# Key norms from turned keys, a value factor on ScalarE and a head factor on GpSimd in a hybrid decoder block

## The chip, the cores and the metric

The kernel runs on one core of a Trainium2 chip. A core has a matrix engine (TensorE, PE in the profile, with its weight loads as PEld), VectorE (DVE), ScalarE (ACT), GpSimd (POOL) and SyncE (SP), which only issues transfers. The metric is the device time of one execution in microseconds.

## The reference

One decoder layer of two token mixers on 512 tokens of width 2048, all in float32. The input is normed to `u`; one projection of `u` gives everything that both mixers need. The first mixer (mLSTM, 8 heads) is not touched here. The second is a gated DeltaNet with 16 heads of 128 channels. Queries, keys and values go through a short causal convolution and SiLU, and queries and keys are divided by their norms. Per head, in chunks:

```
kk    = k k^T
a_mat = strict_lower(beta_t * kk * decay)
sol   = (I + a_mat)^-1 [ v*beta , k*beta*exp(gam) ]
step:   u = w_val - w_k S ;  o = q_dec S + (q k^T * decay) u ;  S = g_end S + k_end^T u
```

The norms of the keys enter `a_mat` and the right-hand side as factors per token. Both mixers' outputs go through a norm and gates, one output projection, a gated sum with the input and a last norm.

## The kernel before, in words

The 32-bit products are split: a weight tile is cast to a high part on ScalarE (`split_hi`, L140), the low part is the difference on VectorE (`split_lo`, L143), and PE runs three matmuls for each pair. Up to L796 the kernel makes most of the projection; after it, eight units (`dn_unit`, L1128) of two heads each run the key, value and query projection of those heads (`proj_cm`, L246). The output projection follows (`wide_block`, then `seven` and `last_block`).

All other work is woven between the projections by Python generators. `tick()` is called after each group of six projection matmuls, 48 times in a unit, and every active generator that is due goes on to its next `yield n`, which says in how many ticks it wants to go on. So a `yield` sets where in PE's order, and in the program order of the other engines, a step stands. PE keeps the order of the program. The other engines' orders are laid out by a planner from a simulated timeline, with `urgent(level)` raising precedence and `behind("A")`, `behind("V")` or `behind("S")` putting an instruction after the newest split on ScalarE, the newest split on VectorE or the newest weight load on SyncE. At run time each engine goes through its list in order.

The steps of a unit that matter here:

- `silu_end` (L840) ends the SiLU of keys, values or queries and calls `turn` (L856), which transposes 32x32 blocks on VectorE and starts `travel` (L863): four writes to DRAM on SyncE's queue, and some ticks later one read back, which completes a transposed tile. The turned keys are `ke`, with tokens on partitions.
- `dn_front_k` (L882) makes decay matrices `dm`, the products `pk` of keys with keys (L915) and `aq` = `pk` * `dm` (L917). It takes the keys' squared norms `nk` from the diagonal of `aq` by four masked sums a head on VectorE (L920), forms `cs` = beta / `nk`, scales `aq` on ScalarE (L935 to L938) and `dm` on GpSimd (L946), sends 32x32 blocks through DRAM to `ls`, and inverts 32 triangular systems at a time in 31 steps of two VectorE instructions (L964, L966), two steps to a tick. The result `xi` goes through DRAM to `tt` (L979) and is turned to `tn` (L982).
- `dn_back` (L1006) builds the full 128x128 inverses in `tb` from 32x32 and 64x64 blocks by four groups of small matmuls, p1 (L1020), p2 (L1035, L1036), p3 (L1046, L1047) and p4 (L1056, L1057), with copies between them on VectorE, ScalarE and GpSimd (`ta` and `tb`). It also multiplies the values `vn` by the keys' norms (`nk`, by then their roots; L1029).
- `dn_chain` (L1065) walks the four chunks of a head, each a few matmuls with VectorE and ScalarE steps between.

`token_norms` (L849) is there already, for the queries:

```
for c in range(NC):
    with urgent():
        A.activation(jk, pk[:, c, :], AF.Square, accum_out=dst[:, c:c + 1])
```

Of the kernel before, what the change touches and what calls it, by code (L numbers as in the profile page):

```python
# [8 lines left out]
F32 = mybir.dt.float32  # L9
F32R = mybir.dt.float32r  # L10
AF = mybir.ActivationFunctionType
ALU = mybir.AluOpType
# [3 lines left out]
P = 128  # L16
S = 512
NC = S // P
# [28 lines left out]
UNITS = list(range(8))  # L47
# [11 lines left out]
def hybrid_body(  # L59
# [18 lines left out]
    V, A, G, T = nc.vector, nc.scalar, nc.gpsimd, nc.tensor  # L78
# [16 lines left out]
    ident = cp.tile([P, P], F32, tag="ident", name="ident")  # L95
# [49 lines left out]
    def behind(eng):  # L145

        return tc.issue_after(newest[eng])
# [65 lines left out]
    def start(gen, wait=0, by=None):  # L213
        active.append([gen, clock["t"] + wait, held["by"] if by is None else by])
# [79 lines left out]
    for c in range(NC):  # L294
        xt = xts[c]
        jk = p0.tile([P, HD], F32, tag="jk", name="jk", bufs=2)
# [524 lines left out]
    def bc(col, n):  # L821
        return col.unsqueeze(2).to_broadcast([P, NC, n])
# [17 lines left out]
    def silu_end(dst, then=None):  # L840
        th = wkb.tile([P, S], F32, tag="th", name="th", bufs=2)
        with behind("A"):
            A.activation(th, dst, AF.Tanh)
        V.scalar_tensor_tensor(out=dst, in0=th, scalar=1.0, in1=dst, op0=ALU.add, op1=ALU.mult)
        if then is not None:
            turn(*then)
        yield 1

    def token_norms(pk, dst):  # L849

        jk = wk.tile([P, P], F32, tag="jk", name="njk", bufs=1)
# [3 lines that stand above are left out]
# [8 lines left out]
    def travel(o, dst, out, apart):  # L863

        d = dst if len(dst.shape) == 4 else dr.tile([16, BS, 4, BS], F32, tag="td", name="td", bufs=8)
        ov = o.rearrange("p n (j c) -> p (n j) c", c=BS)
        if out:
            for a in range(4):
                with behind("A") if out is nc.scalar else ExitStack():
                    out.dma_start(d[:, :, a, :].rearrange("m r c -> r m c"), ov[a * BS:(a + 1) * BS])  # L870
                if apart:
                    yield 1
            return
        with urgent(2):
            for a in range(4):
                nc.sync.dma_start(d[:, :, a, :].rearrange("m r c -> r m c"), ov[a * BS:(a + 1) * BS])
        yield 4
        with urgent(2):
            nc.sync.dma_start(dst, d.rearrange("(n j) r a c -> (j r) n (a c)", n=NC))
        yield 1  # L880

    def dn_front_k(hs, kq, u):  # L882
# [26 lines left out]
        for j in range(2):  # L909
            aq = u["pool"].tile([P, NC, 2, P], F32, tag="aq", name="aq", bufs=2)  # L910
            u["aq"].append(aq)
            pk = psw.tile([P, NC, P], F32, tag="wk", name="pk")
            for c in range(NC):
                tsl = slice(c * P, (c + 1) * P)
                T.matmul(pk[:, c, :], kq[j][:, 0, tsl], kq[j][:, 0, tsl], start=True, stop=True)  # L915
            with urgent():
                V.tensor_tensor(out=aq[:, :, 0, :], in0=pk, in1=u["dm"][j][0], op=ALU.mult)  # L917
                jk = wkb.tile([P, P], F32, tag="jd", name="jd", bufs=1)
                for c in range(NC):
                    V.scalar_tensor_tensor(out=jk, in0=aq[:, c, 0, :], scalar=1.0, in1=ident, op0=ALU.mult,  # L920
                                           op1=ALU.mult, accum_out=nk[:, j, c:c + 1])
            yield 1
        V.tensor_scalar(out=nk, in0=nk, scalar1=EPS, scalar2=None, op0=ALU.add)
        V.reciprocal(cs, nk)
        for j in range(2):
            V.tensor_tensor(out=cs[:, j, :], in0=cs[:, j, :], in1=beta[:, :, hs[j]], op=ALU.mult)
        u["nk"], u["cs"] = nk, cs
        ld = dr.tile([2 * NC, 4, BS, BS], F32, tag="ld", name="ld", bufs=2)
        yield 3
        for j in range(2):  # L930
            aq = u["aq"][j]
            with behind("A"):
# [26 lines left out]
        for i in range(BS - 1):  # L959
            n, m = BS - 1 - i, i // 4 + 1  # L960
            tmp = wkb.tile([P, 80], F32, tag="tmp", name="tmp")
            tv = tmp[:, 0:n * m].rearrange("p (a b) -> p a b", b=n)
            with behind("V"):
                V.tensor_tensor(out=tv, in0=ls[:, i, i + 1:BS].unsqueeze(1).to_broadcast([P, m, n]),  # L964
                                in1=xi[:, 0:m, i].unsqueeze(2).to_broadcast([P, m, n]), op=ALU.mult)
            V.tensor_tensor(out=xi[:, 0:m, i + 1:BS], in0=xi[:, 0:m, i + 1:BS], in1=tv, op=ALU.subtract)  # L966
            if i % 2:
                yield 1
        for j in range(2):
            ke = u["ke"][j]  # L970
# [5 lines left out]
        with urgent():  # L976
            for q in range(4):
                nc.sync.dma_start(xd[:, :, :, q, :].rearrange("g b m t -> (g b) m t"), xi[q * NSYS:(q + 1) * NSYS])
            nc.sync.dma_start(tt, xd.rearrange("g b m q t -> (b m q) g t"))  # L979
        yield 16  # L980
        with urgent(), behind("V"):
            V.transpose(tn.rearrange("p g m -> p (g m)"), tt.rearrange("p g t -> p (g t)"))  # L982
        u.update(tn=tn, tt=tt)
# [22 lines left out]
    def dn_back(hs, kq, u):  # L1006

        tn, tt = u["tn"], u["tt"]
        G2 = [(j * NC + c, u["aq"][j][:, c, 0, :]) for j in range(2) for c in range(NC)]
        for b in range(4):  # L1010
            bs = slice(b * BS, (b + 1) * BS)
            G.tensor_copy(tb[bs, :, bs], tt[bs])
        for b in range(2):
            bs = slice(b * BS, (b + 1) * BS)
            G.tensor_copy(ta[bs, :, bs], tn[bs])
        p1 = psw.tile([P, 2 * NC, BS], F32, tag="wk", name="p1")
        for g, a in G2:
            for q in range(2):
                a0, a1 = slice(64 * q, 64 * q + 32), slice(64 * q + 32, 64 * q + 64)
                T.matmul(p1[a1, g, :], a[a0, a1], tn[a0, g, :], start=True, stop=True)  # L1020
        s1 = wk.tile([P, 2 * NC, BS], F32, tag="s3", name="s1", bufs=1)
        for q in range(2):
            a1 = slice(64 * q + 32, 64 * q + 64)
            with urgent():
                A.mul(s1[a1], p1[a1], -1.0)
        for j in range(2):
            vn = u["vs"][j]
            with behind("V"):
                V.tensor_tensor(out=vn, in0=vn, in1=bc(u["nk"][:, j, :], P), op=ALU.mult)  # L1029
        yield 2  # L1030
        p2 = psw.tile([P, 2, 2 * NC, BS], F32, tag="wk", name="p2")
        for g, a in G2:
            for q in range(2):
                a0, a1 = slice(64 * q, 64 * q + 32), slice(64 * q + 32, 64 * q + 64)
                T.matmul(p2[a0, 0, g, :], s1[a1, g, :], tt[a1, g, :], start=True, stop=True)  # L1035
            T.matmul(p2[32:64, 1, g, :], tt[32:64, g, :], s1[32:64, g, :], start=True, stop=True)  # L1036
        with urgent(2):
            V.tensor_copy(ta[32:64, :, 0:32], p2[32:64, 1])
        for q in range(2):
            a0, a1 = slice(64 * q, 64 * q + 32), slice(64 * q + 32, 64 * q + 64)  # L1040
            with urgent():
                A.copy(tb[a0, :, a1], p2[a0, 0])
        yield 3
        p3 = psw.tile([P, NC, 64], F32, tag="wk", name="p3")
        for c in range(NC):
            T.matmul(p3[64:128, c, :], G2[c][1][0:64, 64:128], ta[:, c, :], start=True, stop=True)  # L1046
            T.matmul(p3[0:64, c, :], G2[NC + c][1][64:128, 0:64], tb[64:128, NC + c, 64:128], start=True, stop=True)  # L1047
        s3 = wk.tile([P, NC, 64], F32, tag="s3", name="s3", bufs=1)
        with urgent():
            A.mul(s3[64:128], p3[64:128], -1.0)  # L1050
            V.tensor_tensor(out=s3[0:64], in0=p3[0:64], in1=u["cs"][0:64, 1, :].unsqueeze(2).to_broadcast([64, NC, 64]),
                            op=ALU.mult)
        yield 3
        p4 = psw.tile([P, NC, 64], F32, tag="wk", name="p4")
        for c in range(NC):
            T.matmul(p4[0:64, c, :], s3[64:128, c, :], tb[64:128, c, 64:128], start=True, stop=True)  # L1056
            T.matmul(p4[64:128, c, :], ta[:, NC + c, :], s3[0:64, c, :], start=True, stop=True)  # L1057
        with urgent():
            V.tensor_copy(tb[0:64, 0:NC, 64:128], p4[0:64])
            A.mul(tb[0:64, NC:2 * NC, 64:128], p4[64:128], -1.0)  # L1060
        soon = hs[0] == 2 * UNITS[-1]
        start(dn_chain(0, hs, kq, u, soon), 3 - soon)
        start(dn_chain(1, hs, kq, u, soon), 4 - soon)
# [64 lines left out]
    def dn_unit(p):  # L1128
# [7 lines left out]
        for j in range(2):  # L1136
            ke = u["pool"].tile([P, NC, P], F32, tag="ke", name="ke", bufs=2)
            u["ke"].append(ke)
            conv_silu(ps[j], 16 + hs[j], kq[j][:, 0, :])
            start(silu_end(kq[j][:, 0, :], (kq[j][:, 0, :], ke)), 4 + 3 * j, front)  # L1140
        start(dn_front_k(hs, kq, u), 1, front)
        ps = proj_cm(DN_V + dcol)
        for j in range(2):
# [641 lines left out]
```

## Time and profile before

| | us |
|---|---|
| median of three runs | 2145.11 |
| lowest and highest of them | 2144.95, 2146.8 |
| the profiled execution, its own time | 2143.23 |
| its span from first to last instruction | 2141.5 |
| PE busy | 2113.5 |
| VectorE busy | 1708.0 |
| ScalarE busy | 1057.6 |
| GpSimd busy | 451.1 |

The granted clock of PE was 0.998 of full speed. In the rows, a line number is that of the kernel, then come the engine, the operation, what it writes and reads, the shapes and a count; behind the first bar the busy time in us and the mean of one in ns, behind the second the idle time of the engine ahead of these instructions and what ended it. A row of waits names who waited for whom, with the total in us, how often and the longest. A row of a timeline begins with the time from the span's start and the duration, and has in brackets the engine's idle time ahead of it. A row of a window gives its length and for PE, PEld, DVE, ACT and POOL the busy time with the count of instructions, then the granted clock, the share of the transfer engines and GB/s. A row on one tile gives shortest, median and longest in ns.

### The profile page before, as it was taken

The numbers are of one execution on the slowest core, as the hardware profiler recorded it, in microseconds if no ns is written. First come the engines' busy times: TensorE is split into PE (matmuls) and PEld (weight loads), VectorE is DVE, ScalarE is ACT, GpSimd is POOL, SyncE is SP. The second block draws the span as 40 slices with busy tenths as digits, with TensorE's granted clock in tenths as the row PEclk, the third lists the DMA queues.
The fourth block names the chain that finished last, engine by engine and source line by source line (L and its number), as shares of the span: only waits on it lengthen the run. The fifth ranks groups of instructions, "written<-read, shape, count | busy, mean of one in ns | idle before, by whom it ended". The sixth has DMA issues, their size and how long they took to land.

```text
span 2141.5 us, 32018 instructions
## 1 busy us (share of the span) xinstructions
PE 2113.5 (99%) x10544; PEld 1752.6 (82%) x10544; DVE 1708.0 (80%) x2981; ACT 1057.6 (49%) x2066; POOL 451.1 (21%) x667
## 2 busy tenths in 40 slices
PE   6999999999999999999999999999999999999998
PEld 5888888888888888888888888888888888887886
DVE  5888888788788778777766887888878878569887
ACT  5444454445444444444445546456465464345345
POOL 0000000000004000000003335344343363233211
PEclk9999999999999999999999999999999999999999
DMA  5355676667677767766766867777686677778895
GB/s 162 119 192 190 212 217 198 220 199 224 206 234 237 245 196 226 240 209 212 253 205 165 208 166 180 183 180 192 182 211 173 171 189 224 196 223 287 245 302 225
DMA packets 447144, 444.21 MB, mean 207 GB/s; under 512 B 197121, under 2 KB 303842, under 8 KB 446850
## 3 DMA queue, kind: packets, MB, share of 16 engines
q1 hardware_dynamic: 377618, 337.22, 53.9%
q0 software_dynamic: 24752, 72.90, 10.9%
q10 hardware_dynamic: 44608, 32.06, 4.8%
q8 instruction: 82, 1.34, 0.3%
q14 instruction: 84, 0.69, 0.1%
HBM read 348.66 MB, written 97.58 MB: 208 GB/s over the span
## 4 chain that ended last, share of the span: by engine, by line
PE 95%; DVE 2%; DMA 2%; issue 1%; SPq 0%; POOL 0%; ACT 0%; DVEq 0%; POOLq 0%; ACTq 0%
PE ps L578 18%; PE ps L580 18%; PE ps L579 18%; PE pj L257 10%; PE pj L259 9%; PE pj L258 9%; PE py L1407 2%; PE py L1409 2%; PE py L1408 2%; PE pk L915 1%; DMA wr<-in_w_out_dram 1%; PE pqk L990 1%; PE pw L1087 1%; PE pnum L1213 1%; PE po L1102 1%
## 5 line engine op out<-in xcount | busy, mean ns | idle before, releaser
L143 DVE TENSOR_TENSOR wl<-wr,wh 128x512 fp32r<-128x512 f32 (+1 forms) x522 | 444.3, 852 | 176.5 <-ACT wh L140 172.3
L140 ACT CAST wh<-wr 128x512 fp32r<-128x512 f32 (+1 forms) x522 | 373.9, 717 | 422.1 <-PE pj L258 218.5
L257 PE MATMUL pj<-uh,wh 128*128 128x512 f32 x896 | 375.8, 419 | 0.0
L259 PE MATMUL pj<-uh,wl 128*128 128x512 f32 x896 | 351.5, 392 | 0.0
L258 PE MATMUL pj<-ul,wh 128*128 128x512 f32 x896 | 349.8, 390 | 0.0
L578 PE MATMUL ps<-wh,uh 128*128 128x512 f32 x752 | 292.7, 389 | 0.8 <-DVE X L632 0.8
L579 PE MATMUL ps<-wl,uh 128*128 128x512 f32 x752 | 292.6, 389 | 0.0
L580 PE MATMUL ps<-wh,ul 128*128 128x512 f32 x752 | 292.6, 389 | 0.0
L140 ACT CAST wh<-t 128x1024 fp32r<-128x1024 f32 x120 | 126.3, 1053 | 301.7 <-PE ps L580 197.5
L533 POOL DMA_DIRECT2D t_d<-ts x104 | 56.6, 544 | 921.8 <-DVE ts L520 853.5
L579 PE MATMUL ps<-wl,suh 128*128 128x512 f32 x624 | 242.9, 389 | 0.0
L580 PE MATMUL ps<-wh,sul 128*128 128x512 f32 x624 | 242.8, 389 | 0.0
L578 PE MATMUL ps<-wh,suh 128*128 128x512 f32 x624 | 242.8, 389 | 0.0
L140 ACT CAST wh<-ts 128x512 fp32r<-128x512 f32 x240 | 147.9, 616 | 184.7 <-DVE ts L538 157.6
L143 DVE TENSOR_TENSOR wl<-t,wh 128x1024 fp32r<-128x1024 f32 x120 | 147.0, 1225 | 81.9 <-ACT wh L140 81.5
L259 PEld LDWEIGHTS pj<-uh,wl 128*128 128x128 f32 x896 | 168.3, 188 | 37.0
L257 PEld LDWEIGHTS pj<-uh,wh 128*128 128x128 f32 x896 | 169.2, 189 | 29.7
L258 PEld LDWEIGHTS pj<-ul,wh 128*128 128x128 f32 x896 | 169.3, 189 | 28.5
L143 DVE TENSOR_TENSOR wl<-ts,wh 128x512 fp32r<-128x512 f32 x240 | 164.9, 687 | 32.6 <-ACT wh L140 31.2
L578 PEld LDWEIGHTS ps<-wh,uh 128*128 128x128 f32 x752 | 141.2, 188 | 30.4 <-DVE X L632 1.2
L579 PEld LDWEIGHTS ps<-wl,uh 128*128 128x128 f32 x752 | 141.2, 188 | 29.5
L580 PEld LDWEIGHTS ps<-wh,ul 128*128 128x128 f32 x752 | 141.2, 188 | 29.2
(345 smaller groups left out, 3804.2 us busy)
## 6 DMA issues: line engine op xcount, KB each, us to landing
wr<-in_w_in_dram SPq DMA_DIRECT2D x744, 256.0 KB, 3.6
wr<-in_w_out_dram SPq DMA_DIRECT2D x138, 256.0 KB, 4.8
t_d<-ts POOLq DMA_DIRECT2D x104, 256.0 KB, 3.6
wr<-t_d SPq DMA_DIRECT2D x104, 256.0 KB, 3.7
xt<-in_x_dram SPq DMA_DIRECT2D x8, 512.0 KB, 7.2
tg_d<-X ACTq DMA_DIRECT2D x16, 256.0 KB, 4.8
tg_d<-to ACTq DMA_DIRECT2D x16, 256.0 KB, 4.6
v<-v_d SPq DMA_DIRECT2D x8, 512.0 KB, 5.6
```

Of the source, the lines that this page charges most:

```text
L140: newest["A"] = A.copy(hi, src).ins
L143: newest["V"] = V.tensor_tensor(out=lo, in0=src, in1=hi.bitcast(F32), op=ALU.subtract).ins
L257: T.matmul(ps[j], hi[:, k, wsl], uh[:, kt, :], start=(kt == 0), stop=False)
L258: T.matmul(ps[j], hi[:, k, wsl], ul[:, kt, :], start=False, stop=False)
L259: T.matmul(ps[j], lo[:, k, wsl], uh[:, kt, :], start=False, stop=(kt == KT - 1))
L533: queue.dma_start(t2_d[b % 2, i], ts[:, 0, :])
L578: T.matmul(ps[t], ah, hi, start=(g == "A" and i == 0), stop=False, skip_group_check=True)
L579: T.matmul(ps[t], ah, lo, start=False, stop=False, skip_group_check=True)
L580: T.matmul(ps[t], al, hi, start=False, stop=(i == KH - 1), skip_group_check=True)
L1407: T.matmul(ps[c], uh[:, kt, tsl], hi, start=(kt == ks[0]), stop=False)
L1408: T.matmul(ps[c], uh[:, kt, tsl], lo, start=False, stop=False)
L1409: T.matmul(ps[c], ul[:, kt, tsl], hi, start=False, stop=(kt == ks[-1]))
```

## The change

Four things change, all in the units. The keys' squared norms no longer come from the diagonal of `aq` but from the turned keys `ke`, by `token_norms` on ScalarE, some ticks later; `cs` and the inverse move with them. In exchange the second head's silu end is started a tick earlier, the read in `travel` comes three ticks after the writes instead of four (for every turned tile that is read back), there are twelve ticks instead of sixteen from the inverse's way out to its turning, and in the last unit four steps of the inverse are issued to a tick. The values' factor goes from VectorE (two instructions) to ScalarE (eight). The second head's factor `cs` is put into the right half of `ta` by GpSimd before p4, instead of into p3's result by VectorE after p3; p3's result is then negated as a whole by ScalarE, and the sign of the last copy changes.

```diff
@@ travel
-        yield 4
+        yield 3
@@ dn_front_k
-                jk = wkb.tile([P, P], F32, tag="jd", name="jd", bufs=1)
-                for c in range(NC):
-                    V.scalar_tensor_tensor(out=jk, in0=aq[:, c, 0, :], scalar=1.0, in1=ident, op0=ALU.mult,
-                                           op1=ALU.mult, accum_out=nk[:, j, c:c + 1])
             yield 1
+        yield 2
+        for j in range(2):
+            with behind("A"):
+                token_norms(u["ke"][j], nk[:, j, :])
+            yield 2 - j
         V.tensor_scalar(out=nk, in0=nk, scalar1=EPS, scalar2=None, op0=ALU.add)
...
-        yield 3
+        yield 2
         for j in range(2):
             aq = u["aq"][j]
...
-            if i % 2:
+            if i % 4 == 3 or (i % 2 and hs[0] < 2 * UNITS[-1]):
                 yield 1
...
-        yield 16
+        yield 12
@@ dn_back
-            with behind("V"):
-                V.tensor_tensor(out=vn, in0=vn, in1=bc(u["nk"][:, j, :], P), op=ALU.mult)
+            with behind("A"):
+                for c in range(NC):
+                    A.mul(vn[:, c, :], vn[:, c, :], u["nk"][:, j, c:c + 1])
...
+        G.tensor_tensor(out=ta[:, NC:], in0=ta[:, NC:], in1=u["cs"][0:64, 1, :].unsqueeze(2).to_broadcast([64, NC, 64]),
+                        op=ALU.mult)
...
-            A.mul(s3[64:128], p3[64:128], -1.0)
-            V.tensor_tensor(out=s3[0:64], in0=p3[0:64], in1=u["cs"][0:64, 1, :].unsqueeze(2).to_broadcast([64, NC, 64]),
-                            op=ALU.mult)
+            A.mul(s3, p3, -1.0)
...
-            A.mul(tb[0:64, NC:2 * NC, 64:128], p4[64:128], -1.0)
+            A.copy(tb[0:64, NC:2 * NC, 64:128], p4[64:128])
@@ dn_unit
-            start(silu_end(kq[j][:, 0, :], (kq[j][:, 0, :], ke)), 4 + 3 * j, front)
+            start(silu_end(kq[j][:, 0, :], (kq[j][:, 0, :], ke)), 4 + 2 * j, front)
```

## The prediction

> **What bounds the kernel now.** I read the page's first part, then TensorE's (PE) waits, then the stages in windows, then who waits for whom in the weight path.
>
> ```profile
> span 2141.5 us, 32018 instructions
> PE 2113.5 (99%) x10544; PEld 1752.6 (82%) x10544; DVE 1708.0 (80%) x2981; ACT 1057.6 (49%) x2066; POOL 451.1 (21%) x667
> ...
> L143 DVE TENSOR_TENSOR wl<-wr,wh 128x512 fp32r<-128x512 f32 (+1 forms) x522 | 444.3, 852 | 176.5 <-ACT wh L140 172.3
> L140 ACT CAST wh<-wr 128x512 fp32r<-128x512 f32 (+1 forms) x522 | 373.9, 717 | 422.1 <-PE pj L258 218.5
> ```
>
> PE stands idle 2141.5 - 2113.5 = 28.0 us. Where:
>
> ```profile
> PE pprm L108 <- POOL rs L304: 14.6, 1, 14.6
> PE put L313 <- DVE xt L290: 2.1, 2, 1.3
> PE ps L578 <- DVE X L632: 0.8, 1, 0.8
> PE ps L578 <- DVE X L1431: 0.7, 2, 0.5
> PE pw L1087 <- DVE r L1082: 0.3, 1, 0.3
> ```
>
> ```profile
> 0.00:25.00 25.00, 8.33 (x38) 6.94 (x38) 13.89 (x29) 14.68 (x21) 3.26 (x14) 1.00 0.78 238
> 1204.00:1290.00 86.00, 85.70 (x529) 71.50 (x527) 72.56 (x194) 49.23 (x138) 29.95 (x45) 1.00 0.68 171
> 2130.00:2141.50 11.50, 2.08 (x10) 1.39 (x8) 4.43 (x10) 3.75 (x6) 1.08 (x2) 0.71 0.67 274
> ```
>
> The start holds 25.00 - 8.33 = 16.67 us, the last stretch 11.50 - 2.08 = 9.42 us. What is left is 28.0 - 16.67 - 9.42 = 1.91 us: 0.30 us in the eight DeltaNet units, which the change touches, and about 1.6 us where the output products begin. The change therefore works on engines that PE does not wait for. The two group rows say the same from the other side: ScalarE's weight split (L140) is held up mostly by PE giving buffers back (218.5 of its 422.1 us idle), so the splits run ahead as far as the buffers let them. Nothing in the units can be gained that PE does not lose now: the ceiling is 1.91 us, 0.09%.
>
> **The clock of the units.** Work beside the projections is issued in ticks, 48 to a unit. Two pieces of the chain of waits, one unit apart:
>
> ```profile
> 1399.60 0.89 PE pk L915 x8
> ...
> 1485.48 0.89 PE pk L915 x8
> ```
>
> 85.88 us / 48 = 1.79 us a tick. I count ticks from the end of a unit's key projection. Before: key products at 8 and 9, factors `cs` at 10, `aq` scaled at 13 and 14, inverse from 24 to 39, turned inverse `tn` at 55, back part at 57 (61 in the last unit). After: products at 8 and 9, norms at 12 and 14, `cs` at 15, `aq` scaled at 17 and 18, inverse from 28 to 43 (28 to 35 in the last unit), `tn` at 55 (47), back part at 57 (61). Every tick at which PE gets work is the same, and no matmul is added or removed: PE's own time is unchanged, and only new waits or lost waits can move the end.
>
> **The change part by part.** The prices:
>
> ```profile
> L920 DVE SCALAR_TENSOR_TENSOR jd<-aq,ident 128x128 f32<-128x128 f32 x64 | 19.5, 305 | 1.1
> L920 DVE DVE_READ_ACCUMULATOR jd<-aq,ident 128x1 f32 x64 | 5.3, 83 | 0.0
> L1029 DVE TENSOR_TENSOR vt<-vt,nk 128x512 f32<-128x512 f32 x16 | 10.3, 685 | 0.0
> L1051 DVE TENSOR_TENSOR s<-p,cs x8: 408/416/417, 1241.9 to 1840.8; 64x256 f32<-64x256 f32 x8
> L854 ACT ACTIVATE njk<-qn 128x128 f32<-128x128 f32 x64 | 19.8, 310 | 1.6
> L854 ACT ACTIVATION_READ_ACCUMULATOR njk<-qn 128x1 f32 x64 | 12.0, 187 | 0.0
> L938 ACT ACTIVATE aq<-aq,cs 128x128 f32<-128x128 f32 x32 | 10.2, 390 | 0.0
> L946 POOL TENSOR_TENSOR dm<-dm,cs 128x512 f32<-128x512 f32 x16 | 16.9, 1071 | 0.0
> ```
>
> *VectorE loses,* a unit: 8 x (0.305 + 0.083) + 2 x 0.685 + 0.416 = 4.9 us. Worth on PE's path: 0 to 0.3 us over the kernel, since the one wait of a unit's matmul for VectorE is 0.3 us; I take 0.
>
> *ScalarE gains* the eight squares with their accumulator reads, (19.8 + 12.0) / 64 = 0.50 us each, 4.0 us, and eight products of 128x128 at 10.2 / 32 = 0.32 us, 2.55 us: 6.5 us a unit. The negation of p3 only grows from 64 to 128 partitions, at the same 256 elements each, so I take it as unchanged. The squares at ticks 12 and 14 and the value products from tick 9 of the next unit fall into one stretch: the back part of a unit (its ticks 57 to 65) is the next unit's 9 to 17. In the stretch from 1401.80 (tick 9):
>
> ```profile
> 1401.80:1408.25 6.45, 6.45 (x107) 5.34 (x107) 6.08 (x21) 2.48 (x7) 1.12 (x3) 1.00 0.77 198
> 1408.25:1413.30 5.05, 5.05 (x36) 3.98 (x35) 1.64 (x8) 4.99 (x17) 5.03 (x7) 1.00 0.96 262
> 1413.30:1420.00 6.70, 6.70 (x43) 5.31 (x43) 6.67 (x10) 4.37 (x8) 5.20 (x9) 1.00 0.57 153
> ```
>
> ScalarE (fourth busy figure) has 18.20 - 2.48 - 4.99 - 4.37 = 6.36 us free there, and 6.5 us come in. That is just full. What gives is the scaling of `aq`, moved to ticks 17 and 18: its reader is the inverse, ten ticks on. What must not be late are the steps that PE needs:
>
> ```profile
> 1408.25 0.74 ACT L1042 COPY tb<-p 32x256 f32<-32x256 f32 x2 [2.83 <-DVE ta L1038]
> ...
> 1411.23 0.27 PE L1046 MATMUL p<-ta,aq 64*64 64x64 f32 x1
> ...
> 1415.47 0.41 DVE L1051 TENSOR_TENSOR s<-p,cs 64x256 f32<-64x256 f32 x1
> ...
> 1415.84 0.39 PE L259 MATMUL pj<-uh,wl 128*128 128x512 f32 x1
> 1416.15 0.27 PE L1056 MATMUL p<-tb,s 64*64 64x64 f32 x1
> ```
>
> The copy into `tb` ends at 1408.99, 2.24 us ahead of p3, and ScalarE had waited 2.83 us ahead of it: the value products (2.55 us) fit into that very hole. The step on VectorE that goes (L1051) ended at 1415.88, only 0.27 us ahead of p4; ScalarE's negation takes its place. So the tightest step gets more room, and the `tb` copy gets less. On PE's path: 0, if ScalarE keeps the copy within 2.24 us; this cover is what rival A takes away.
>
> In sentences of their own: the Trainium skill, "ScalarE: Activation LUTs", Rules for kernel authors, says that a multiplication belongs on VectorE rather than ScalarE. By that rule the value factor is moved the wrong way, and the rows agree on the engine's time (2.55 us against 1.37 us a unit); carried to the end, the 1.2 us would add 9.4 us in eight units. By the trace it adds nothing, as ScalarE has the hole and PE does not wait for it.
>
> *GpSimd gains* one 64x256 product a unit. The nearest row, a 128x512 product with the same broadcast, takes 1.07 us; half the elements give 0.54 us, the whole 1.07 us is the upper end; I take 0.54. It follows VectorE's copy into `ta`, due by p4, five ticks later (9 us). Its place in GpSimd's queue is behind whatever waits there; at tick 15 the `dm` products stood, which now come at 19, so the place is cleared by the same change. Cost 0; if it waits out the 9 us, PE waits for all beyond.
>
> *Turned keys earlier.* The second head's silu end comes one tick earlier, and each read back of a turned tile follows its writes after three ticks instead of four.
>
> ```profile
> td<-ke SPq DMA_DIRECT2D x64, 64.0 KB, 2.7
> ke<-td SPq DMA_DIRECT2D x16, 256.0 KB, 3.8
> ```
>
> Three ticks are 5.4 us, the writes need 2.7 us and the read 3.8 us, so keys are there before ticks 12 and 14 with 1.6 us to spare. The read waits on SyncE's queue in order, and weight loads stand behind it; at worst a load is 1.79 us later, under a split that itself waits for PE. Values and queries are read a tick earlier too, with the same answer. Cost 0; with no cover, 1.79 us a read.
>
> *The inverse four ticks later, with twelve ticks instead of sixteen after it.* In unit 3 and in the last unit:
>
> ```profile
> 1459.96 0.17 DVE L966 TENSOR_TENSOR xi<-xi,tmp 128x8 f32<-128x8 f32 x1
> ...
> 1471.39 2.26 POOL L1012 COPY tb<-tt 32x256 f32<-32x256 f32 x4 [3.17 <-DMA tt<-xd]
> ...
> 1483.80 0.44 DVE L982 STREAM_TRANSPOSE tn<-tt 128x256 f32<-128x256 f32 x1
> ...
> 1816.24 0.17 DVE L966 TENSOR_TENSOR xi<-xi,tmp 128x8 f32<-128x8 f32 x1
> ...
> 1827.95 0.45 DVE L982 STREAM_TRANSPOSE tn<-tt 128x256 f32<-128x256 f32 x1 [5.28 <-DMA tt<-xd]
> ...
> 1830.28 0.41 PE L1020 MATMUL p<-tn,aq 32*32 32x32 f32 x14
> ```
>
> In unit 3 the way out and back takes 1471.39 - 1460.13 = 11.3 us; 7.2 us later it ends at 1478.6, 5.2 us before VectorE turns it. In the last unit `tn` is already late: VectorE stands 5.28 us for the transfer, and PE's use follows 1.88 us after. There the inverse begins 7.2 us later but is issued four steps to a tick instead of two, and would end four ticks earlier if VectorE kept pace. Bounds for PE: 0 to 7.2 - 1.88 = 5.3 us. I take 0, since VectorE's load falls and the issue is denser.
>
> *Sum:* 2143.23 us for the profiled execution (span 2141.5 and 1.7 around it) + 0 + 0 + 0 + 0 + 0. The median of the runs shown is 1.9 us above the profiled time; I keep that offset and take off 0.2 us, half of what the 0.3 us wait and the tight p4 could give: **2144.9 us**.
>
> **The rivals.**
>
> A, slower: ScalarE's order breaks the back part. If all 6.5 us stood ahead of the `tb` copy, it would be late by 6.5 - 2.83 = 3.7 us, and PE would wait 3.7 - 2.24 = 1.5 us a unit: 2145.1 + 8 x 1.5 = 2157 us. It decides from 2.24 us of delay, and is told from no change from 2.8 us (0.54 us of stall a unit). For it: 6.5 us into 6.36 us, squares that are put ahead of other work, and keys that may land late with ScalarE's queue standing behind them. Against: copy and negation have the same precedence and their inputs come first.
>
> B, slower: in the last unit the inverse keeps its whole 7.2 us: PE waits 5.3 us, 2150.4 us. For it: VectorE waits for this transfer already. Against: denser issue.
>
> C, faster: all 1.91 us of waits after the start go: 2143.2 us. For it: the lighter VectorE is the engine named in each of them. Against: 1.6 us of them lie after the units, where the change does nothing. It is within 0.2%.
>
> D: more than 4.3 us faster. Nothing in the rows allows it; left for what the rows hide.
>
> E, slower: GpSimd's new product holds VectorE up. In these rows a split of a unit took 1.57 us, against a mean of 0.852 us for this line, while GpSimd's products ran:
>
> ```profile
> 1412.26 2.03 POOL L946 TENSOR_TENSOR dm<-dm,cs 128x512 f32<-128x512 f32 x2
> ...
> 1413.27 1.57 DVE L143 TENSOR_TENSOR wl<-wr,wh 128x512 fp32r<-128x512 f32 x1 [2.91 <-ACT wh L140]
> ```
>
> The new product could hold a split or a step for its own 0.54 us once a unit: 8 x 0.54 = 4.3 us, 2149.4 us, if PE stood right behind it. Against: PE had no wait in this stretch, with products four times as large. The Trainium skill, "SBUF — State Buffer", Who interferes with whom, has the mechanism: a VectorE instruction with two SBUF inputs blocks against a GpSimd instruction that reads SBUF. By that rule the new product blocks a split wholly, and the trace agrees on the lock.
>
> **How the numbers follow.** No change or less than 0.2% (4.3 us, about what a measurement of this kernel can tell): 0.85, of which C 0.10. A 0.07, B 0.02, E 0.02: slower 0.11. D 0.04. Below 2143.0 I leave 0.05; above 2149.5, where A decides in full, 0.08. So 2143.0 to 2149.5.
>
> **What would show it.** VectorE busy near 1708 - 39 = 1669 us and ScalarE near 1110 us, with PE still at 2113 us. PE's waits: no row for p, pw or pj over 0.5 us. If A: rows for p3 (L1046) or p4 behind ScalarE, some microseconds in total. If B: one wait of the last unit's L1020 for `tn`. Wrong altogether if the units take a period other than 85.9 us, or if PE's busy time itself moves.

## Result, and the profile after

The changed kernel takes 2173.48 us (median of 4 runs, 2170.70 to 2177.77), against 2145.03 us for the kernel before beside it (2143.58 to 2146.80): a ratio of 1.0134, interval 1.0115 to 1.0153. It is 28.45 us slower, far outside the range that was forecast. The profiled execution took 2174.86 us.

The first part of the page after, and TensorE's waits:

```profile
span 2172.8 us, 32077 instructions
PE 2121.6 (98%) x10544; PEld 1756.9 (81%) x10544; DVE 1705.5 (78%) x2829; ACT 1098.5 (51%) x2258; POOL 441.9 (20%) x675
```

```profile
PE p L1021 <- DVE tn L983: 10.0, 2, 8.7
PE p L1037 <- ACT s L1026: 6.9, 8, 2.0
...
PE ps L578 <- DVE X L1433: 1.5, 1, 1.5
PE pnum L1217 <- DVE c L1227: 1.4, 1, 1.4
...
PE pk L915 <- DVE aq L917: 1.2, 1, 1.2
```

The span grew by 2172.8 - 2141.5 = 31.3 us. PE's idle time grew from 28.0 to 2172.8 - 2121.6 = 51.2 us, by 23.2: 10.0 us of waits for `tn`, 6.9 us for `s1` (the negated copy of p1 on ScalarE, read by p2), and a number of waits of about 1 us. The other 8.1 us are PE's own busy time, with the same 10544 matmuls. Windows of the trace after show where it grew (behind the five engines stands the granted clock):

```profile
1204.00:1290.00 86.00, 75.57 (x459) 62.56 (x459) 60.32 (x142) 48.02 (x136) 28.45 (x44) 0.94 0.61 155
...
1233.50:1243.70 10.20, 4.76 (x45) 4.34 (x46) 1.14 (x2) 1.76 (x5) 3.40 (x13) 0.50 0.23 47
1513.40:1516.80 3.40, 3.40 (x9) 2.62 (x9) 2.42 (x4) 3.07 (x13) 0.96 (x2) 0.51 0.57 177
```

Three stretches in the units ran at half the clock: 10.2 us from 1233.5, 3.4 us from 1513.4, and another 3.4 us from 1602.1. PE was busy for 4.76 + 3.40 + 3.39 = 11.55 us of them. By my estimate about half of that is loss, 5.8 of the 8.1 us; where the other 2.3 us lie is not traced.

**The first unit's `tn`.** The one long wait, in the timelines of VectorE and PE:

```profile
1238.35 0.45 DVE L983 STREAM_TRANSPOSE tn<-tt 128x256 f32<-128x256 f32 x1 [7.48 <-DMA tt<-xd]
...
1238.94 1.06 PE L1021 MATMUL p<-tn,aq 32*32 32x32 f32 x32 [8.70 <-DVE tn L983]
```

One part of this is that the inverse itself ended late. Its last step on VectorE, in the kernel before:

```profile
1212.22 0.18 DVE L966 TENSOR_TENSOR xi<-xi,tmp 128x8 f32<-128x8 f32 x1
1212.30 0.75 DVE L837 SCALAR_TENSOR_TENSOR kq<-yp,convc,kq 128x512 f32<-128x512 f32 x1
```

and the end of the inverse after:

```profile
1216.72 0.74 DVE L837 SCALAR_TENSOR_TENSOR kq<-yp,convc,kq 128x512 f32<-128x512 f32 x1
...
1224.51 0.13 DVE L967 TENSOR_TENSOR xi<-xi,tmp 128x8 f32<-128x8 f32 x1
```

Before, the key convolution of the next unit (`kq`, L837) followed the inverse's last step. After, it begins with three pairs of steps still to go, and these stand one by one between the convolution, the SiLU and the turning of the next unit's keys in VectorE's list. The inverse began 6.1 us later than before, took 43.0 us for 36.9, and ended 12.2 us later.

The other part is SyncE's queue, which shows why `tt` came later still; first the kernel before, then after:

```profile
1212.55 2.62 SPq L978 DMA_DIRECT2D xd<-xi  x4
...
1216.65 0.37 SPq L979 DMA_DIRECT2D tt<-xd  x1
```

```profile
1224.61 4.14 SPq L876 DMA_DIRECT2D td<-ke  x8
...
1229.90 0.68 SPq L979 DMA_DIRECT2D xd<-xi  x1
...
1233.17 0.56 SPq L979 DMA_DIRECT2D xd<-xi  x1
...
1236.00 0.36 SPq L980 DMA_DIRECT2D tt<-xd  x1
```

Before, the four stores of the inverse went out at 1212.55, and `tt` was asked for at 1216.65. After, the inverse was done at 1224.6, but in SyncE's list its stores now stand behind the eight key writes of the next unit and partly behind the reads of those keys: the first store went at 1229.90, 5.3 us after its data, the last at 1233.17, and `tt` at 1236.00.

**Every unit's inverse ends later than its four ticks.** In unit 3 of the trace after, the last step of the inverse, and p1, which stands at the same tick as before:

```profile
1491.62 0.13 DVE L967 TENSOR_TENSOR xi<-xi,tmp 128x8 f32<-128x8 f32 x1
...
1501.09 2.39 POOL L1013 COPY tb<-tt 32x256 f32<-32x256 f32 x4 [2.32 <-DMA tt<-xd]
...
1506.20 0.69 PE L1021 MATMUL p<-tn,aq 32*32 32x32 f32 x32
```

From the inverse's end to p1 there are 14.5 us. Before, it was 1487.67 - 1460.13 = 27.5 us (the inverse's last row stands in the prediction; p1's row is below), so the inverse ends 13 us later against PE, not 7.2. In this unit p1 did not wait for it: `tt` landed at 1501.09, and VectorE turned it at 1505.24. The same stretch of the inverse in windows, before and after:

```profile
1427.80:1460.00 32.20, 32.20 (x179) 27.71 (x178) 29.16 (x96) 14.74 (x41) 3.05 (x4) 1.00 0.56 142
```

```profile
1451.30:1491.00 39.70, 39.70 (x211) 33.99 (x210) 35.55 (x99) 16.74 (x48) 11.18 (x14) 1.00 0.59 153
```

The inverse takes 40 us instead of 32 (the second window ends just short of its last step). GpSimd is busy for 11.18 us beside it instead of 3.05: four ticks later the inverse runs into the stretch in which GpSimd works on the gates and queries, and VectorE's instructions stretch there. This does not explain the first unit, where GpSimd was busy for 13.7 us beside the inverse and for 14.9 us before. From the timeline of unit 3 after, GpSimd and VectorE:

```profile
1482.59 3.43 DVE L143 TENSOR_TENSOR wl<-wr,wh 128x512 fp32r<-128x512 f32 x1
...
1483.17 1.30 POOL L996 TENSOR_TENSOR kq<-kq,gb 128x512 f32<-128x512 f32 x1
1484.42 1.04 POOL L1124 TENSOR_TENSOR gz<-gz,rsd 128x512 f32<-128x512 f32 x1
```

One weight split took 3.43 us (0.68 where GpSimd rests), and the inverse's next step had to wait behind it. The same is seen in a group on VectorE that the change does not touch, the values' convolution, into which the `dm` and `ke` products on GpSimd now fall; groups of before, then after:

```profile
L837 DVE SCALAR_TENSOR_TENSOR vt<-yp,convc,vt 128x512 f32<-128x512 f32 x48 | 37.6, 801 | 1.0 <-ACT vt L835 1.0
```

```profile
L837 DVE SCALAR_TENSOR_TENSOR vt<-yp,convc,vt 128x512 f32<-128x512 f32 x48 | 54.3, 1140 | 4.2 <-ACT vt L835 4.0
```

That is 16.7 us more for the same 48 instructions; the inverse's own steps (L965, L967) took 9.9 us more. VectorE lost 152 instructions, as the change says, and its busy time fell by 2.5 us only, not by 39. The Trainium skill, "SBUF — State Buffer", Who interferes with whom, says that VectorE's second pair of ports is GpSimd's only one, under an exclusive lock; by that rule an instruction of VectorE that needs both pairs waits for GpSimd, and these rows agree.

**`s1` behind the value products.** ScalarE and PE in unit 3, before and after:

```profile
1487.67 0.69 PE L1020 MATMUL p<-tn,aq 32*32 32x32 f32 x32
...
1488.42 0.78 ACT L1025 ACTIVATE s<-p 32x256 f32<-32x256 f32 x2 [0.27 <-PE p L1020]
```

```profile
1507.67 0.40 ACT L1031 ACTIVATE vt<-vt,nk 128x128 f32<-128x128 f32 x1
...
1508.44 1.28 ACT L1031 ACTIVATE vt<-vt,nk 128x128 f32<-128x128 f32 x4
...
1511.70 0.77 ACT L1026 ACTIVATE s<-p 32x256 f32<-32x256 f32 x2
...
1512.12 0.24 PE L1037 MATMUL p<-tt,s 32*32 32x32 f32 x2 [1.41 <-ACT s L1026]
```

Before, ScalarE stood ready for p1 and copied it 0.75 us after p1's start. After, the products and masks that stand ahead of `s1` in its list run from 1507.67 on, and `s1` starts 5.5 us after p1's start. It costs PE 1.4 to 2.2 us in each of units 2 to 5.

### The profile page after: what moved, and what is told of

It reads as the page before. It is cut to its first block, busy times and chain, and to the rows that moved or that the text cites. A ratio compares the mean times of both kernels' runs of the same rounds, so it can differ in the third digit from the quotient of the medians.

```text
span 2172.8 us, 32077 instructions
## 1 busy us (share of the span) xinstructions
PE 2121.6 (98%) x10544; PEld 1756.9 (81%) x10544; DVE 1705.5 (78%) x2829; ACT 1098.5 (51%) x2258; POOL 441.9 (20%) x675
## 4 chain that ended last, share of the span: by engine, by line
PE 79%; DVE 8%; ACT 5%; DMA 4%; issue 2%; SPq 1%; POOL 0%; ACTq 0%; DVEq 0%; POOLq 0%
PE ps L579 17%; PE ps L578 17%; PE ps L580 17%; PE pj L257 6%; PE pj L258 6%; PE pj L259 6%; DVE wl L143 2%; PE py L1409 1%; PE py L1411 1%; PE py L1410 1%; DVE xi L967 1%; DMA wr<-in_w_in_dram 1%; DVE tmp L965 1%; ACT wh L140 1%; ACT njk L854 1%
## 5 line engine op out<-in xcount | busy, mean ns | idle before, releaser
L143 DVE TENSOR_TENSOR wl<-t,wh 128x1024 fp32r<-128x1024 f32 x120 | 146.9, 1224 | 82.4 <-ACT wh L140 81.8
```

Source lines behind the costliest of these rows:

```text
L143: newest["V"] = V.tensor_tensor(out=lo, in0=src, in1=hi.bitcast(F32), op=ALU.subtract).ins
```

## The experiments

Three suspects came out of this reading: the late inverse (with SyncE's order), the value products ahead of `s1`, and the half clock that follows both. All kernels compute the whole function. In the shifts below, a unit's place is the start of its first key product, against the same unit of the kernel before; units count from 0.

| | unit 1 | unit 2 | unit 3 | unit 5 | unit 7 |
|---|---|---|---|---|---|
| the change | 1.5 | 14.9 | 16.8 | 22.1 | 27.9 |
| value factor back on VectorE | 0.8 | 14.0 | 17.0 | 17.1 | 17.9 |
| late inverse alone | 1.1 | 8.9 | 10.1 | 10.3 | 10.9 |
| value factor back, inverse two ticks later | 2.5 | 9.9 | 11.4 | 11.4 | 11.1 |

**Undoing one part.** The value factor back on VectorE, then the first unit's inverse four steps to a tick, then both:

```diff
@@ value factor, on the changed kernel
-            with behind("A"):
-                for c in range(NC):
-                    A.mul(vn[:, c, :], vn[:, c, :], u["nk"][:, j, c:c + 1])
+            with behind("V"):
+                V.tensor_tensor(out=vn, in0=vn, in1=bc(u["nk"][:, j, :], P), op=ALU.mult)
@@ first unit's inverse, on the changed kernel
-            if i % 4 == 3 or (i % 2 and hs[0] < 2 * UNITS[-1]):
+            if i % 4 == 3 or (i % 2 and 0 < hs[0] < 2 * UNITS[-1]):
```

> The changed kernel with one part undone: the values' factor is again two VectorE instructions. Theory: the eight value products stand in ScalarE's queue ahead of the copy of p1 (s1), and p2 waits for it; so the waits of p2 for s1 (6.9 us in the changed kernel) go, the wait of p1 for tn in the first back part (8.7 us) stays, and the time falls from 2173.5 to 2158 to 2163 us. Rival: it is the squares of the keys that fill ScalarE, and the value products only stand beside them; then p2 still waits and the time stays within 3 us of 2173.5.

Measured 2163.1 us, ratio 1.0082 (1.0067 to 1.0097), 10.4 us less than the change (11.6 us, when each is set against the kernel before of its own round). No wait for `s1` is left, and the shifts hardly move from unit 3 on (17.0 to 17.9): the products are what made the middle units late. The wait for `tn` in the first unit stays at 8.6 us.

> The changed kernel with the first unit's inverse issued four steps to a tick as in the last unit, so that it ends four ticks before that of the kernel before would. Theory: the first wait of p1 for tn (8.7 us) and the half clock behind it go, 2159 to 2163 us; p2's waits for s1 stay. Rival: the way of the inverse through DRAM is what is late, whatever its start; then more than half of the 8.7 us stays and the time is over 2167 us.

Measured 2175.81 us, ratio 1.0137 (1.0122 to 1.0152), nothing gained: the inverse ended at 1224 as in the change, and PE waited 8.9 us. The density of issue is not what ends the inverse; this guess fell.

> The changed kernel with both: value factor on VectorE and the first unit's inverse dense. Theory: the two causes add, 2146 to 2151 us, with no wait over 0.5 us for s1 or tn before the last unit. If it stays over 2155 us, there is a third cause among what is left (key squares on ScalarE, reads a tick earlier, GpSimd's product).

Measured 2163.74 us, ratio 1.0085 (1.0070 to 1.0100), the same as with the value factor alone. The wait for `tn` in the first unit stayed at 8.5 us, so this run cannot tell whether there is a third cause.

**One part alone.** The value factor alone on the kernel before (the edit above, the other way round), the inverse's time alone, and the second head's factor alone:

```diff
@@ inverse's time, on the kernel before
-        yield 3
+        yield 7
...
-        yield 16
+        yield 12
@@ second head's factor, on the kernel before
+        G.tensor_tensor(out=ta[:, NC:], in0=ta[:, NC:], in1=u["cs"][0:64, 1, :].unsqueeze(2).to_broadcast([64, NC, 64]),
+                        op=ALU.mult)
...
-            A.mul(s3[64:128], p3[64:128], -1.0)
-            V.tensor_tensor(out=s3[0:64], in0=p3[0:64], in1=u["cs"][0:64, 1, :].unsqueeze(2).to_broadcast([64, NC, 64]),
-                            op=ALU.mult)
+            A.mul(s3, p3, -1.0)
...
-            A.mul(tb[0:64, NC:2 * NC, 64:128], p4[64:128], -1.0)
+            A.copy(tb[0:64, NC:2 * NC, 64:128], p4[64:128])
```

> The kernel before with one part alone: the values' factor as eight ScalarE products. Theory: p2 waits for s1 by 1 to 2 us in most units, 2150 to 2158 us. Rival (the squares fill ScalarE): no wait, 2144 to 2147 us.

Measured 2149.19 us, ratio 1.0015 (1.0005 to 1.0024): 3.0 us, between the two ranges, and not at the expected place. In unit 3 `s1` ended 0.8 us ahead of p2. The delay went another way: the masks on ScalarE (L901) came behind the products, VectorE's `aq` waited for them, with it the keys' norms and `cs`; ScalarE's scaling of `aq` waited 1.07 us for `cs`, the weight cast behind it came late, VectorE stood 2.50 us for that cast, and the step on p3 (`s3`) behind VectorE. PE waited for `s3` in units 1 and 4, 1.3 us each; in unit 3, which shows the same chain, it came just in time. PE's waits, and then VectorE's timeline in unit 3:

```profile
PE p L1058 <- DVE s L1052: 2.5, 2, 1.3
```

```profile
1493.48 0.69 DVE L917 TENSOR_TENSOR aq<-pk,dm 128x512 f32<-128x512 f32 x1 [1.59 <-ACT dm L901]
...
1501.85 0.69 DVE L143 TENSOR_TENSOR wl<-wr,wh 128x512 fp32r<-128x512 f32 x1 [2.50 <-ACT wh L140]
...
1504.77 0.42 DVE L1052 TENSOR_TENSOR s<-p,cs 64x256 f32<-64x256 f32 x1
```

> The kernel before with one thing of the change alone: the inverse, and what it needs, stands four ticks later in every unit (four more ticks ahead of the scaling of aq, four fewer ahead of tn). Norms, value factor and the second head's factor stay as they were. Theory now (the later inverse is the larger cause, since in unit 0 its four tiles are stored behind the next unit's eight key writes on SyncE's queue): PE waits 7 to 10 us for tn in unit 0, PE's busy time rises by 3 to 6 us at half clock behind it, and p1 in the later units waits for little; 2155 to 2162 us, no wait of p2 for s1. Rival (it is the norms on ScalarE that make the inverse late, not its four ticks): the wait for tn in unit 0 is below 2 us, and the time is 2145 to 2149 us. Rival of the prediction's own step (7.2 us later, of which 5.2 are free): 2145 to 2150 us.

Measured 2157.97 us, ratio 1.0056 (1.0041 to 1.0071): 11.75 us for the late inverse by itself. The time is inside the theory's range; its parts are not: PE waited 4.3 us for `tn` in the first unit, not 7 to 10, and its busy time rose by 6.4 us, not 3 to 6. VectorE's busy time rose as well, from 1708.0 to 1735.5 us for the same 2981 instructions, and in unit 3 the inverse took 40.5 us for 32.4: the later place alone makes it longer. PE's wait for `tn`, and SyncE's timeline with the read of `tt` behind key writes again:

```profile
PE p L1020 <- DVE tn L982: 6.7, 2, 4.3
```

```profile
1228.48 2.36 SPq L876 DMA_DIRECT2D td<-ke  x4
1230.94 0.45 SPq L979 DMA_DIRECT2D tt<-xd  x1
```

PE ran 6.8 us at half clock from 1233.1. From unit 3 on the shift hardly moves (10.1 to 10.9): between the units, the late inverse costs only where the first meets the second. The span is 15.1 us longer, though, and the other 4.2 us come behind the last unit's key products, for the most part at its p1, the place of rival B:

```profile
1843.66 0.83 PE L1020 MATMUL p<-tn,aq 32*32 32x32 f32 x32 [2.40 <-DVE tn L982]
```

There PE waited 2.40 us for `tn` and then ran 3.4 us at half clock.

> The kernel before with one part of the change alone: the second head's inverse factor put in by GpSimd (one product of 64 x 256 a unit, measured at 0.61 us), and the first head's sign folded as in the change. All theories: no wait of PE that was not there before and 2144 to 2147 us; the prediction put 0.54 to 1.07 us of GpSimd's time a unit behind it and nothing on the path. If GpSimd's product stops VectorE for its length at a place that matters, 2149 to 2151 us (0.6 us in each of eight units).

Measured 2147.41 us, ratio 1.0009 (1.0000 to 1.0019). GpSimd's product took 0.605 to 0.628 us. 1.9 us is within what can't be told from no change, and no single wait carries it. VectorE's busy time rose all the same, from 1708.0 to 1716.6 us, although its eight instructions of 0.4 us went away.

Alone the three cost 3.0 + 11.75 + 1.9 = 16.7 us; together with the norms on ScalarE, which weren't run by themselves, 28.45.

**The inverse back at its old tick.** With the whole change otherwise, and with the value factor back as well. As the twelve ticks behind the inverse stay, `tn` is turned four ticks earlier than in the kernel before:

```diff
-        yield 9
+        yield 5
         for i in range(BS - 1):
```

> The changed kernel with the inverse back at its old tick: five ticks instead of nine between the norms' factor and the first step of the inverse's substitution, everything else as changed. Theory now: the tiles of unit 0's inverse stand ahead of the key writes on SyncE's queue again, its wait for tn goes, with the half clock behind it (-11 to -14 us); the waits of p2 for s1 in units 3 to 6 stay, since the value products still stand ahead of s1 on ScalarE: 2158 to 2163 us. Rival (the waits for s1 come from a late tn, not from the value products): both go, 2146 to 2150 us. Rival (unit 0's inverse is held up by ScalarE's norms): nothing changes, 2172 to 2176 us.

Measured 2161.23 us, ratio 1.0078 (1.0062 to 1.0095). The time lies in the theory's range (2158 to 2163 us) by luck: the waits for `s1`, which it said would stay, went too, as its first rival had it, and new waits came instead:

```profile
PE pr L1081 <- DVE st L1100: 3.3, 2, 2.3
PE pw L1089 <- DVE r L1084: 2.2, 3, 1.0
...
PE p L1037 <- ACT s L1026: 0.2, 1, 0.2
```

In unit 3 the value products started at 1494.57, about with p1 (1494.4), where in the change they start 1.5 us after it. So the late inverse also makes `s1` late. The likely link, which no run isolates, is that it pushes VectorE's other work back, with it the queries' norms and the masks on ScalarE, and with those the products.

> Both suspected causes undone: the changed kernel with the value factor back on VectorE and the inverse at its old tick. What stays of the change: the norms from the turned keys on ScalarE, the second head's factor by GpSimd, the turned keys earlier. Theory now: 2146 to 2150 us, no PE wait for tn over 2 us and none for s1; what is left of the change is worth within 0.2% of the kernel before. If a third cause stands behind the two, the time is over 2152 us and a wait of PE names it. If the change's gain on VectorE had been hidden by the two, it is below 2143 us.

Measured 2158.49 us, ratio 1.0064 (1.0044 to 1.0083): a third cause. VectorE's waits point to it:

```profile
DVE tmp L965 <- DMA ls<-ld: 22.2, 7, 4.6
```

In the kernel before this was 5.9 us (3 times, 2.3 at most). The norms come four to five ticks later, so `ls` lands later, and an inverse at its old tick stands at the head of VectorE's list without data; the state steps of the chains (`st`, `r`) stand behind it. This cost is my experiment's: the change had moved the inverse for that reason.

**Two ticks instead of four.** With the value factor back, and with the whole change:

```diff
-        yield 9
+        yield 7
         for i in range(BS - 1):
```

> The changed kernel with the value factor back on VectorE and the inverse two ticks later than before instead of four (seven ticks between the norms' factor and the substitution, where the change has nine and the inverse-early run has five). The inverse-early run ended 12 us over the kernel before, with VectorE waiting 22.2 us for ls to land, up to 4.6 us at a time, at the first step of the inverse, and with the state steps behind it late. Theory now: two ticks, 3.6 us, cover most of that wait, so the waits of PE for st and r fall under 2 us in all, and unit 0's tiles still stand ahead of the key writes on SyncE: 2146 to 2152 us; then the change has no fixed time for the inverse that is free, only less wrong ones. Rival (the norms on ScalarE or the factor on GpSimd hold up the state steps by themselves): the waits for st and r stay at 5 to 7 us, 2156 to 2160 us.

Measured 2159.68 us (2154.58 to 2160.38), ratio 1.0060 (1.0045 to 1.0075). The waits for `ls` fell to 5.7 us, those for `st` are gone, and by the shifts the units from 3 on cost nothing (11.4 to 11.1). This trace is of the fastest execution, 2154.58 us; the other three took 2159.5 to 2160.4, and where they lost the 5 us no trace shows. The loss is at the first unit again, as PE's waits and SyncE's timeline show:

```profile
PE p L1021 <- DVE tn L983: 4.1, 1, 4.1
```

```profile
1224.33 0.56 SPq L979 DMA_DIRECT2D xd<-xi  x1
1224.99 2.17 SPq L876 DMA_DIRECT2D td<-ke  x4
...
1231.08 0.47 SPq L980 DMA_DIRECT2D tt<-xd  x1
```

> The whole change, with the inverse two ticks later than before instead of four. Theory now (with the inverse at its old tick the waits for s1 went to 0.2 us although the value products stood ahead of s1, and what remained were VectorE's waits for ls): no wait of p2 for s1 over 1 us, the state steps late by less than in the inverse-early run, 2148 to 2157 us. Rival (the value products hold up s1 unless the inverse is fully early): 1 to 2 us a unit in four units for s1, 2157 to 2163 us.

Measured 2174.49 us, ratio 1.0134 (1.0119 to 1.0149). The rival held for the waits, and the time is beyond both ranges: 8.1 us of waits for `s1`, and six stretches of 3.4 or 6.8 us at half clock in the units and behind them. Between the two runs of this pair stand the value products alone: 14.8 us. PE's waits with the whole change:

```profile
PE p L1037 <- ACT s L1026: 8.1, 10, 2.5
```

**Another place for the products.** Issued behind the first copies into `tb`:

```diff
@@ ahead of p2
-        for j in range(2):
-            vn = u["vs"][j]
-            with behind("A"):
-                for c in range(NC):
-                    A.mul(vn[:, c, :], vn[:, c, :], u["nk"][:, j, c:c + 1])
         yield 2
...
@@ ahead of p3
+        for j in range(2):
+            vn = u["vs"][j]
+            with behind("A"):
+                for c in range(NC):
+                    A.mul(vn[:, c, :], vn[:, c, :], u["nk"][:, j, c:c + 1])
```

> The changed kernel with the value products still on ScalarE, but issued behind the first copies into tb, ahead of the product p3, instead of behind s1's second half. Theory now (the products' place in ScalarE's queue, not their amount, holds up s1): the waits of p2 for s1 go; the wait for tn in unit 0 and the half clock stay; 2160 to 2167 us if nothing stands in the new place, and 2168 to 2176 with a new wait (p3 for tb, or p4 for s3, 1.5 to 2.7 us in each of 4 to 6 units) if ScalarE's queue has no free place there. Rival (ScalarE's amount of work is what matters): the waits for s1 stay at 1 to 2 us each.

Measured 2170.63 us, ratio 1.0115 (1.0100 to 1.0131). No wait for `s1`, so their place made those; but six waits for state steps (`PE pr L1081 <- DVE st L1100`, 5.2 us in all) took over. Neither of the two places tried on ScalarE is free.

**The first unit: the queue or the time.** The stores and the read of `tt` issued by GpSimd in the first unit only, with four ticks and with two; and the first unit at its old tick with the others at two (value factor on VectorE in all three):

```diff
+        dq = nc.gpsimd if hs[0] == 2 * UNITS[0] else nc.sync
         with urgent():
             for q in range(4):
-                nc.sync.dma_start(xd[:, :, :, q, :].rearrange("g b m t -> (g b) m t"), xi[q * NSYS:(q + 1) * NSYS])
-            nc.sync.dma_start(tt, xd.rearrange("g b m q t -> (b m q) g t"))
+                dq.dma_start(xd[:, :, :, q, :].rearrange("g b m t -> (g b) m t"), xi[q * NSYS:(q + 1) * NSYS])
+            dq.dma_start(tt, xd.rearrange("g b m q t -> (b m q) g t"))
@@ the third run
-        yield 9
+        yield 5 if hs[0] == 2 * UNITS[0] else 7
```

> The changed kernel with the value factor back on VectorE, and in unit 0 alone the four stores of the inverse's tiles and the read of tt issued by GpSimd instead of SyncE, so that they do not stand behind the next unit's key writes; the inverse is as late as the change has it. Theory now (5 us of unit 0's wait of 8.6 are the queue, 3.6 the late inverse): the stores are issued within 1 us of the inverse's end near 1224, tt lands 4 to 6 us earlier, the wait for tn falls to 2 to 5 us, and half clock behind it to 0 to 7 us: 2154 to 2160 us, against 2163.1 with SyncE. Rival (the inverse's end alone decides): the wait for tn stays over 7 us, 2161 to 2165 us.

Measured 2162.41 us, ratio 1.0079 (1.0064 to 1.0094). The first unit's wait for `tn` fell from 8.6 to 4.6 us and half clock behind it from 10.2 to 6.8 us: by these two traces SyncE's order is 4.0 of the 8.6 us. The median does not tell this from the run with SyncE (2163.1); the expected 2154 to 2160 us was too low.

> The changed kernel with the value factor back on VectorE and the inverse two ticks later in all units; in the first unit alone the stores of the inverse's tiles and the read of tt are issued by GpSimd. Theory now (with two ticks the tiles were on chip 1225.0 and the read of tt stood behind key writes until 1231.1): the read of tt is issued by 1226, lands by 1230, PE's wait for tn of 4.1 us and the half clock behind it go, 2147 to 2153 us. Rival (the late time of the inverse is enough): the wait stays over 2 us and the time over 2155 us.

Measured 2159.55 us, ratio 1.0072 (1.0057 to 1.0087). The wait for `tn` is gone, `tt` was asked for at 1226.33, and the time did not move: another wait stands at p1, for VectorE's `aq`, and 3.4 us at half clock follow it.

```profile
PE p L1022 <- DVE aq L917: 2.9, 1, 2.9
```

> The changed kernel with the value factor back on VectorE; the first unit's inverse at its old tick, the inverse of the others two ticks later than before. Theory now (the other units cost nothing at two ticks, and the first unit's loss is its inverse, which ends behind the key writes on SyncE): no wait of PE for tn over 1 us, no half clock before the end, the key projection of the third unit within 6 us of the kernel before's place (9.8 us late with two ticks in all units), and 2147 to 2152 us. Rival (the norms themselves hold up the first unit): the third unit starts 9 us late or more, 2155 to 2160 us.

Measured 2154.87 us, ratio 1.0042 (1.0029 to 1.0054), the best of the versions with the norms on ScalarE. No wait for `tn`, no half clock before the end, the third unit 7.8 us late; the place and the time both lie between the two theories. What is left is spread over small waits for VectorE:

```profile
PE pnum L1216 <- DVE c L1226: 4.1, 4, 2.1
```

These last 9.5 us have no single cause that I could name; the norms on ScalarE, for which VectorE stands 8.5 us in this run (0 before), are the likely one, which is argued and not shown, as no run takes them alone. No version beats the kernel before.

## Why the prediction was wrong

- *What bounds the kernel* was read rightly: PE was the bound, and nothing could be gained. Off PE's path, though, is not free: every step that PE reads has a time from which it costs, and the part that followed checked that time at too few places.
- *The inverse four ticks later* is the step that failed most (11.75 us alone, 10.0 us of waits in the change and most of the half clock). "7.2 us later it ends at 1478.6, 5.2 us before VectorE turns it" took the inverse's own length as fixed. In unit 3 it grew from 32 to 40 us, beside GpSimd's work, and ended 13 us later against PE; even so `tt` landed 4.1 us before VectorE turned it, close to the 5.2 forecast. The working looked at unit 3 and the last unit only, and the cost fell on the first. There the inverse's last steps stand among the next unit's key convolution on VectorE, it ended 12.2 us later, and its way out stands behind eight key writes on SyncE. The prediction spoke of weight loads behind the key reads, and not of the inverse's stores behind the key writes. Rival B, for the last unit, was real and small: 1.3 us for 5.3 in the change, and 2.4 us with half clock behind it where the inverse was late alone and not issued more densely.
- *ScalarE*: "the value products (2.55 us) fit into that very hole" named a hole ahead of the copy into `tb`, but in the list the products stand ahead of `s1`, whose hole was 0.27 us. Rival A's mechanism came true one copy earlier, at p2 in place of p3 (6.9 us for its 12), with a chance of 0.07 that was far too small. From the rule of the Trainium skill, "ScalarE: Activation LUTs", Rules for kernel authors, that a multiplication belongs on VectorE, the prediction had worked out 9.4 us by engine time. The products cost 3.0 us alone and 10.4 in the change. Engine time would make the two equal; the traces show that what stands behind the products in ScalarE's list decides.
- *VectorE loses 4.9 us a unit*: the instructions went, the time did not (1705.5 us, not 1669). The values' convolution (16.7 us) and the inverse (9.9 us), now beside other work of GpSimd, took most of it back; the rest is not traced. Rival E had the mechanism, and named the new product, the smallest of GpSimd's moved work. The product took 0.61 us for 0.54; alone it raised VectorE's busy time by 8.6 us and the kernel's time by no more than can be told from nothing.
- *Turned keys earlier* was set at 0, and no run took it alone.
- Half clock had no place in the sum: about 5.8 us in the profiled execution.
- The prediction's own sign of being wrong altogether came true: PE's busy time moved, from 2113.5 to 2121.6 us, and from unit 2 on the units took 87.5 to 89.5 us each in place of 85.9.

## What to carry to other kernels

When a step is moved, price its length again from the work that stands beside its new place, on its own engine and on GpSimd, and follow each of its transfers through the program order of the queue in the first, a middle and the last round, not in a middle one alone. Work given to an idle engine costs what stands behind it in that engine's list: find the reader of the very next instructions there, not the mean idle time. Where TensorE is the bound, a wait of a microsecond or two can cost more than itself, through the clock.

## What was not expected of the hardware

Half clock came after short waits. In the change PE waited 1.41 us for `s1`, ran small 32x32 products for about 1 us, and the next matmuls of 128x512 ran at half clock for 3.4 us. PE's timeline after the row at 1512.12 above:

```profile
1513.15 0.65 PE L257 MATMUL pj<-uh,wh 128*128 128x512 f32 x1
1513.59 0.63 PE L258 MATMUL pj<-ul,wh 128*128 128x512 f32 x1
```

They start 0.43 us apart, where ten like them shortly before stood 0.23 apart. The waits for `s1` at 1424.38 (1.20 us) and at 1691.50 (1.99 us, the longest) in the same run were followed by no such stretch. The Trainium skill, "TensorE: Matmul & The Clock Gate", Part 1, says that the clock halves after an idle window of about 3.4 us, free-running, and gives as its rule no idle gaps above about 3.4 us. The lengths here (3.4, 6.8 and 10.2 us) agree with that window. The gaps do not: a wait under half a window was followed by half clock. Nor are the small products needed for it. A wait of 1.50 us for `X` between 128x512 products, in the output projection, stands in the traces of all twelve kernels with the norms on ScalarE; half clock followed it in two of them (with the whole change at two ticks, where it ended at 1969.11, and with the first unit's tiles issued by GpSimd, at 1955.08). That fits a window that runs freely; no trace shows the window itself, and what else decides is open.
